# Three-pass split products for the attention and convolution output projections, LayerNorm on token rows, and another order of loading x, in an encoder kernel

## The chip, the cores and the metric

The kernel runs on one NeuronCore of a Trainium2 chip. The metric is the device time of one execution in microseconds (us); before the change it is 1177.25 us, the median of three runs (1176.48 to 1177.78). TensorE (PE) multiplies matrices and transposes; VectorE (DVE), ScalarE (ACT) and GpSimd (POOL) work element by element; SyncE (SP) and ACT issue DMAs here. Each engine takes its instructions in a fixed order. SBUF is the working memory, PSUM the memory into which PE writes; both have 128 partitions.

## The reference

Two layers over 256 tokens of width 1024, all in float32. One layer computes:

```
h = x + 0.5 * swiglu(rms_norm(x, norm_ffn1), w_ffn1_in, w_ffn1_out)
u = rms_norm(h, norm_mix)
q, k, v, c, g = split(u @ w_in)                 # 512, 128, 128, 1024, 2048 columns
y_attn = window_attention(norm(q), norm(k), v, sink, rel_bias) @ w_attn_out
c = c_val * sigmoid(c_gate)
c = depthwise_conv(c, conv_w) + conv_b          # 31 taps, 512 channels
c = silu(layer_norm(c, conv_ln_g, conv_ln_b))   # over the 512 channels of a token
y_conv = c @ w_conv_out
h = h + (sigmoid(g_attn) * y_attn + sigmoid(g_conv) * y_conv) @ w_o
h = h + 0.5 * swiglu(rms_norm(h, norm_ffn2), w_ffn2_in, w_ffn2_out)
x = h + (p @ w_pe_proj) * sigmoid(rms_norm(h, norm_pe) @ w_pe_gate)
```

The feed-forward width is 2816. The two matrices that the change touches, `w_attn_out` and `w_conv_out`, are 512 x 1024.

## The kernel before

Activations lie transposed: channels on the partitions, the 256 tokens along the free axis, so that a matrix with 1024 input channels is eight steps of 128 (k) and each product writes 128 output channels by 256 tokens.

Most matrices are multiplied in three passes of float32r (`mm3`): a weight and an activation are each held as a high part, the float32r rounding, and a low part, the rest, and high x high, high x low and low x high are added up in PSUM. The weights' parts are made on the way: `load_upto` issues the DMA of a unit of about 1 MB into one of four raw buffers (on SP, line L76 in the profile), and `prep_upto` casts a tile on ACT (`w_hi`, L100) and subtracts on DVE (`w_lo`, L101), into one of seven buffers each. Such a tile is 128 x 1024 and is called a spec. Preparation runs up to six specs ahead (`LOOK`), and a buffer comes free when PE has used it. The two output projections are the exception: their specs are raw (`raw_spec`), and `products` multiplies them in plain fp32.

The program text does not fix the order on the engines. A scheduler of the framework takes the instructions by priority on a modelled timeline and writes out one order per engine; the convolution's taps on DVE have a low priority (`BACKGROUND`), and the weights' preparation in the mixer has one between (`WEIGHTS_LAG`). In the first section of the program ACT and DVE keep the order of the text (`manual_schedule`).

The stages that the change touches:

- The start. x comes in four DMAs of 256 columns into `x_ld`, which is one of the four raw buffers. PE transposes it (`ps_xt`), ACT multiplies by the gain and rounds (`x0h`), DVE makes the rest (`x0l`), both engines copy it to `x32`. The gains come by a DMA of ACT into `rows_first` and through one more transposition (`ps_par`) into `par`. ACT squares `x32` block by block (`sq`), POOL adds the squares up (`sq_acc`), and a product with a constant matrix gives the mean square for all partitions (`ps_stat`). That product stands in PE's order among the first feed-forward products (`ps_gu`).
- The mixer's tail, once per layer. PE computes the gates (`ps_g`) while attention's scores, softmax and values are worked off between them and DVE runs the 124 convolution taps (L607, tile `y`). Then come four groups of the attention projection (`ps_ao`, each 256 output channels), four groups of the convolution projection (`ps_co`), and `w_o` (`ps_wo`). Between the `ps_ao` groups lies the LayerNorm of the convolution: a product with a constant matrix gives the mean (`ps_mu`), DVE subtracts it, ACT squares, a second product gives the variance (`ps_var`), then square root, reciprocal, product and Silu.

PSUM tiles named by `mm_tile` come from four buffers, those named by `at_tile` from two larger ones.

## Time and profile before

| what | number |
|---|---|
| median of three runs | 1177.25 us (1176.48 to 1177.78) |
| the profiled execution, its span | 1176.52 us, 1174.7 us |
| PE, DVE, ACT, POOL busy | 98%, 69%, 52%, 8% of the span |
| first `ps_gu` product | at 10.76 us |
| layer 0: first `ps_ao`, first `ps_co`, first `ps_wo` | at 313.55, 333.97 and 348.05 us |
| layer 1: first `ps_ao`, first `ps_co`, first `ps_wo` | at 889.83, 909.94 and 924.02 us |
| mean granted clock of TensorE | 0.999 |

In rows of the timeline the first number is the start in us from the span's start, the second the length; then engine, line, operation, tile written <- tiles read, shape, count, and in brackets the idle time before with what ended it. Rows of the windows give a stretch, its length, then busy time and count of PE, PE's weight loads, DVE, ACT and POOL, then granted clock, DMA share and GB/s. In a group of the page the busy sum and the mean in ns stand before the idle time. A busy PE is not PE at its peak: a matmul's record is longer than the distance to the next.

### The profile page before, as it was taken

Reading aid. Unit: us, or ns where it says so; the run is one execution under the profiler, and the core shown is the slowest. Engines: PE = TensorE matmul, PEld = TensorE weight load, DVE = VectorE, ACT = ScalarE, POOL = GpSimd, SP = SyncE. Lnnn points to the kernel's source line nnn. Section 1 sums busy time; section 2 is a strip of 40 time slices with the busy share of each in tenths; the row PEclk is TensorE's granted clock in tenths of the full one; section 3 lists DMA queues with packets and bytes.
Section 4 is the critical chain, followed back from the end, with each engine's and each line's share of the span. In section 5 each row is a group of like instructions: output and inputs, shape, how many; then the busy total and the mean of one; then the engine's idle time right before and its main releaser. Section 6 shows DMA issues by size and latency. Waiting matters only on the chain.

```text
span 1174.7 us, 21809 instructions
## 1 busy us (share of the span) xinstructions
PE 1156.8 (98%) x9082; PEld 1121.5 (95%) x9082; DVE 813.6 (69%) x1214; ACT 614.2 (52%) x1033; POOL 88.5 (8%) x119
## 2 busy tenths in 40 slices
PE   7999999999999999999999999999999999999997
PEld 7999999998889999999999999999987999999997
DVE  5866656798667766656876666569976786666564
ACT  6644444676356544444664444457753564444443
POOL 3000001211002000001110000113000010000110
PEclk9999999999999999999999999999999999999999
DMA  8866556545074565556556464566522664654541
GB/s 252 265 229 209 167 178 200 179 147 141 2 249 161 189 200 175 171 165 214 188 166 204 156 205 152 170 213 193 145 72 68 219 224 159 201 168 144 192 144 37
DMA packets 195694, 202.99 MB, mean 173 GB/s; under 512 B 3731, under 2 KB 188899, under 8 KB 195596
## 3 DMA queue, kind: packets, MB, share of 16 engines
q1 hardware_dynamic: 195564, 201.60, 53.6%
q8 instruction: 71, 1.16, 0.4%
q14 instruction: 27, 0.22, 0.1%
q10 hardware_dynamic: 32, 0.01, 0.0%
HBM read 200.53 MB, written 1.06 MB: 172 GB/s over the span
## 4 chain that ended last, share of the span: by engine, by line
PE 96%; DVE 2%; DMA 1%; ACT 1%; issue 0%; SPq 0%; ACTq 0%
PE ps_gu L313 14%; PE ps_gu L311 14%; PE ps_gu L312 14%; PE ps_fo L313 7%; PE ps_fo L312 7%; PE ps_fo L311 7%; PE ps_g L311 3%; PE ps_g L313 3%; PE ps_g L312 3%; PE ps_co L847 2%; PE ps_s L755 1%; PE ps_c L311 1%; PE ps_pe L313 1%; PE ps_pe L312 1%; PE ps_pe L311 1%; PE ps_c L313 1%
## 5 line engine op out<-in xcount | busy, mean ns | idle before, releaser
L101 DVE TENSOR_TENSOR w_lo<-raw,w_hi 128x1024 fp32r<-128x1024 f32 (+1 forms) x368 | 440.9, 1202 | 241.5 <-ACT w_hi L100 237.4
L100 ACT CAST w_hi<-raw 128x1024 fp32r<-128x1024 f32 (+1 forms) x368 | 377.2, 1030 | 427.0 <-PE ps_gu L312 215.3
L313 PE MATMUL ps_fo<-h_hi,w_lo 128*128 128x256 f32 x704 | 198.6, 283 | 0.0
L312 PE MATMUL ps_fo<-h_lo,w_hi 128*128 128x256 f32 x704 | 198.6, 283 | 0.0
L311 PE MATMUL ps_fo<-h_hi,w_hi 128*128 128x256 f32 x704 | 198.6, 283 | 0.0
L313 PEld LDWEIGHTS ps_fo<-h_hi,w_lo 128*128 128x128 f32 x704 | 134.9, 192 | 0.0
L311 PEld LDWEIGHTS ps_fo<-h_hi,w_hi 128*128 128x128 f32 x704 | 134.9, 192 | 0.0
L312 PEld LDWEIGHTS ps_fo<-h_lo,w_hi 128*128 128x128 f32 x704 | 134.9, 192 | 0.0
L400 POOL TENSOR_TENSOR sq_acc<-sq_acc,sq 128x256 f32<-128x256 f32 x56 | 56.5, 1010 | 903.4 <-ACT sq L399 902.9
L311 PE MATMUL ps_gu<-x0h,w_hi 128*128 128x256 f32 x352 | 100.8, 286 | 2.1 <-ACT x L456 2.1
L607 DVE SCALAR_TENSOR_TENSOR y<-cpad,cw,y 128x256 f32<-128x256 f32 x240 | 101.1, 477 | 0.1
L313 PE MATMUL ps_gu<-x0h,w_lo 128*128 128x256 f32 x352 | 100.4, 285 | 0.2 <-DVE w_lo L101 0.2
L312 PE MATMUL ps_gu<-x0l,w_hi 128*128 128x256 f32 x352 | 100.2, 285 | 0.0
L311 PE MATMUL ps_gu<-xn0h,w_hi 128*128 128x256 f32 x352 | 99.8, 284 | 0.0
L312 PE MATMUL ps_gu<-xf0l,w_hi 128*128 128x256 f32 x352 | 99.8, 284 | 0.0
L312 PE MATMUL ps_gu<-xf1l,w_hi 128*128 128x256 f32 x352 | 99.8, 284 | 0.0
L311 PE MATMUL ps_gu<-xf0h,w_hi 128*128 128x256 f32 x352 | 99.7, 283 | 0.0
L311 PE MATMUL ps_gu<-xf1h,w_hi 128*128 128x256 f32 x352 | 99.7, 283 | 0.0
L313 PE MATMUL ps_gu<-xf0h,w_lo 128*128 128x256 f32 x352 | 99.6, 283 | 0.0
L313 PE MATMUL ps_gu<-xn0h,w_lo 128*128 128x256 f32 x352 | 99.6, 283 | 0.0
L312 PE MATMUL ps_gu<-xn0l,w_hi 128*128 128x256 f32 x352 | 99.6, 283 | 0.0
L313 PE MATMUL ps_gu<-xf1h,w_lo 128*128 128x256 f32 x352 | 99.6, 283 | 0.0
(222 smaller groups left out, 2718.6 us busy)
## 6 DMA issues: line engine op xcount, KB each, us to landing
raw<-in_w_ffn_in_dram SPq DMA_DIRECT2D x86, 1024.0 KB
raw<-in_w_in_dram SPq DMA_DIRECT2D x30, 1024.0 KB
raw<-in_w_ffn_out_dram SPq DMA_DIRECT2D x32, 896.0 KB
raw<-in_w_ffn_out_dram SPq DMA_DIRECT2D x16, 1024.0 KB
raw<-in_w_o_dram SPq DMA_DIRECT2D x8, 1024.0 KB
raw<-in_w_pe_gate_dram SPq DMA_DIRECT2D x8, 1024.0 KB
raw<-in_w_attn_out_dram SPq DMA_DIRECT2D x8, 512.0 KB
raw<-in_w_conv_out_dram SPq DMA_DIRECT2D x4, 1024.0 KB
```

Of the source, the lines that this page charges most:

```text
L100: nc.scalar.copy(out=hv[:, :, d0 : d0 + w], in_=src),
L101: nc.vector.tensor_tensor(out=lv[:, :, d0 : d0 + w], in0=src, in1=hv[:, :, d0 : d0 + w].bitcast(F32), op=ALU.subtract,),
L311: nc.tensor.matmul(ps, wh[:, k0 + k, cols], xh[:, kx, :], start=f, stop=False)
L312: nc.tensor.matmul(ps, wh[:, k0 + k, cols], xl[:, kx, :], start=False, stop=False)
L313: nc.tensor.matmul(ps, wl[:, k0 + k, cols], xh[:, kx, :], start=False, stop=e)
L400: nc.gpsimd.tensor_tensor(out=self.acc, in0=self.acc, in1=sq, op=ALU.add)
L607: nc.vector.scalar_tensor_tensor(out=y[:, i, :], in0=src, scalar=w, in1=y[:, i, :], op0=ALU.mult, op1=ALU.add)
L755: nc.tensor.matmul(ps[:, c, :], qT[v * HD : (v + 1) * HD, c, qb * P : (qb + 1) * P], kT[v * HD : (v + 1) * HD, :], start=True, stop=True,)
L847: nc.tensor.matmul(ps[:, c * T : (c + 1) * T], w[:, k, c * P : (c + 1) * P], x[:, k, :], start=k == 0, stop=k == KC - 1,)
```

## The change

The two projections get split weights like all others, and their inputs are split as well: attention's output `o` when it leaves PSUM, the convolution's output after Silu (`y_h`, `y_l`). `products` calls `mm3`. LayerNorm goes by token rows: PE transposes `y` into two PSUM tiles of 128 tokens by 512 channels (`ps_yt`), DVE takes mean and variance per row (`bn_stats`, `bn_aggr`), normalises into `yn`, and PE transposes back (`ps_yc`), from where ACT applies Silu with gain and bias. It is called one attention group later in its second half (before the fourth instead of the third). At the start two of the four x loads are issued by ACT, two neighbouring k share a PSUM tile, the copies to `x32` come after the splits in pieces of 512, and the first weight spec is prepared after the fifth k. A scratch area of the DMA software is made smaller (1024), and the constant matrix of the mean is gone.

```diff
-        nc.sync.dma_start(x_ld[:, :, s], xv[:, :, s])
+        (nc.sync if i % 2 == 0 else nc.scalar).dma_start(x_ld[:, :, s], xv[:, :, s])
...
             for c in range(2):
-                ws.raw_spec(u, KC, c * 256, 256)
+                ws.spec(KC, 256, [(u, 0, c * 256, 0, 256)])
...
-        def keep_x(k):
-            copy = nc.scalar.copy if k % 2 else nc.vector.tensor_copy
-            copy(out=x32[:, k, :], in_=xT[k])
         for k in range(KD):
-            xT[k] = (mm_tile if 2 <= k < 6 else at_tile)("ps_xt")[:, :T]
+            if k % 2 == 0:
+                xT[k // 2] = mm_tile("ps_xt").rearrange("p (k t) -> p k t", k=2)
+            src = xT[k // 2][:, k % 2, :]
...
-            if k >= 2:
-                keep_x(k - 2)
-        ws.prep_upto(0)
-        keep_x(KD - 2)
-        keep_x(KD - 1)
+            if k == 4:
+                ws.prep_upto(0)
         ws.prep_upto(1)
+        for k in range(0, KD, 2):
+            copy = nc.scalar.copy if k % 4 else nc.vector.tensor_copy
+            copy(out=x32[:, k : k + 2, :], in_=xT[k // 2])
...
-                    nc.scalar.copy(out=o[:, :, qb * P : (qb + 1) * P], in_=ov[:, :, ::-1])
+                    split([p[:, :, qb * P : (qb + 1) * P] for p in o], ov[:, :, ::-1])
...
                 for c in range(2):
-                    for k in range(KC):
-                        nc.tensor.matmul(
-                            ps[:, c * T : (c + 1) * T], w[:, k, c * P : (c + 1) * P], x[:, k, :],
-                            start=k == 0, stop=k == KC - 1,
-                        )
+                    mm3(ps[:, c * T : (c + 1) * T], w, x, cols=slice(c * P, (c + 1) * P))
...
+            def ln_by_token():
+                mv = tmp.tile([P, 2, 2], F32, name="mv")
+                ps = []
+                for t in range(2):
+                    ps.append(mm_tile("ps_yt"))
+                    for i in range(KC):
+                        nc.tensor.transpose(ps[t][:, i * P : (i + 1) * P], y[:, i, t * P : (t + 1) * P], ident)
+                    six = tmp.tile([P, 6], F32, name="six")
+                    nc.vector.bn_stats(out=six, in_=ps[t])
+                    nc.vector.bn_aggr(out=mv[:, t, :], in_=six)
+                rs = tmp.tile([P, 2], F32, name="rs")
+                nc.scalar.activation(out=rs, in_=mv[:, :, 1], func=AF.Sqrt, bias=eps5)
+                nc.vector.reciprocal(out=rs, in_=rs)
+                table(AF.Silu)
+                for t in range(2):
+                    nc.vector.tensor_scalar(
+                        out=yn[:, t, :], in0=ps[t], scalar1=mv[:, t, 0:1], scalar2=rs[:, t : t + 1],
+                        op0=ALU.subtract, op1=ALU.mult,
+                    )
+
+            def ln_by_channel():
                 for i in range(0, KC, 2):
...
+                    ps = mm_tile("ps_yc").rearrange("p (f t) -> p f t", f=2)
+                    for f in range(2):
+                        for t in range(2):
+                            nc.tensor.transpose(
+                                ps[:, f, t * P : (t + 1) * P], yn[:, t, (i + f) * P : (i + f + 1) * P], ident
+                            )
+                    for f in range(2):
+                        nc.scalar.activation(
+                            out=y[:, i + f, :], in_=ps[:, f, :], func=AF.Silu,
+                            scale=pcol("conv_ln_g", l, i + f), bias=pcol("conv_ln_b", l, i + f),
+                        )
+                    split([p[:, i : i + 2, :] for p in yp], y[:, i : i + 2, :])
             for i in range(KC):
                 if i == 1:
-                    ln_mean()
-                if i == 2:
-                    ln_scale()
+                    ln_by_token()
+                if i == 3:
+                    ln_by_channel()
```

The scheduler's orders differ at three places.

ACT at the start, before (L180 loads the gains, L464 makes `x0h`, L456 copies to `x32`, L396 and L399 square):

```order
L180 DMA rows_first<-in_norm_ffn_dram 16x128
L191 ACT_TABLE_LOAD
L191 COPY par<-ps_par 128x16
L464 ACTIVATE x0h<-ps_xt,par 128x256 x4
L456 COPY x_99<-ps_xt 128x256
L464 ACTIVATE x0h<-ps_xt,par 128x256 x2
L456 COPY x_99<-ps_xt 128x256
L464 ACTIVATE x0h<-ps_xt,par 128x256 x2
L456 COPY x_99<-ps_xt 128x256
L100 CAST w_hi<-raw 128x1024
```

and now (L460 makes `x0h`, L469 copies):

```order
L166 DMA x_ld<-in_x_dram 128x2x256 x2
L180 DMA rows_first<-in_norm_ffn_dram 16x128
L191 ACT_TABLE_LOAD
L191 COPY par<-ps_par 128x16
L460 ACTIVATE x0h<-ps_xt,par 128x256 x5
L100 CAST w_hi<-raw 128x1024
L460 ACTIVATE x0h<-ps_xt,par 128x256 x3
L100 CAST w_hi<-raw 128x1024
L469 COPY x_97<-ps_xt 128x512
L100 CAST w_hi<-raw 128x1024 x2
L469 COPY x_97<-ps_xt 128x512
L394 ACTIVATE sq_acc<-x_97 128x256
```

Two loads of x stand ahead of the gains' load, the first cast stands after five `x0h` instead of eight, and four casts and the copies stand ahead of the first square, where two stood before. On PE `ps_par` now follows eight of the sixteen `ps_xt`, and the last two `ps_xt` stand after the first nineteen `ps_gu` products; the `ps_xt` of an odd k wait for the `x0l` of the even k in the same tile. On SP the DMA of the fourth weight unit waits for the first `w_lo`, and that of the fifth for the last `ps_xt`; before, it was the other way round.

DVE at the mixer's tail of layer 0, before (L607 are taps, L828 gates leaving PSUM, L857 an attention group leaving PSUM, L868 the subtraction of the mean):

```order
L828 TENSOR_TENSOR g<-ps_g,r_x 128x512
L607 SCALAR_TENSOR_TENSOR y<-cpad,cw,y 128x256 x6
L857 TENSOR_TENSOR g<-ps_ao,g 128x512
L607 SCALAR_TENSOR_TENSOR y<-cpad,cw,y 128x256 x2
L857 TENSOR_TENSOR g<-ps_ao,g 128x512
L868 TENSOR_TENSOR y<-y,ps_mu 128x512 x2
L101 TENSOR_TENSOR w_lo<-raw,w_hi 128x1024 x2
```

and now (L603 are taps, L849 an attention group):

```order
L101 TENSOR_TENSOR w_lo<-raw,w_hi 128x1024
L603 SCALAR_TENSOR_TENSOR y<-cpad,cw,y 128x256 x2
L849 TENSOR_TENSOR g<-ps_ao,g 128x512
L101 TENSOR_TENSOR w_lo<-raw,w_hi 128x1024
L603 SCALAR_TENSOR_TENSOR y<-cpad,cw,y 128x256 x17
L864 BN_STATS six<-ps_yt 128x6 x2
L865 BN_AGGR mv<-six 128x2 x2
L868 RECIPROCAL rs<-rs 128x2
L871 TENSOR_SCALAR yn<-ps_yt,mv,rs 128x512 x2
L849 TENSOR_TENSOR g<-ps_ao,g 128x512
L443 TENSOR_TENSOR y_l<-y,y_h 128x512
```

Seventeen taps now stand behind the third attention group, where none did. From the last `w_lo` of the gates on, the order has ten `w_lo` ahead of these taps; before, it had none between the gates' last and the taps' end.

PE at the same place, before (L847 are projection products in fp32, L866 and L876 mean and variance):

```order
L847 MATMUL ps_ao<-o,raw 128x256 x2
L866 MATMUL ps_mu<-y,ones_c 128x256
L876 MATMUL ps_var<-ysq,ones_c 128x256 x2
L847 MATMUL ps_ao<-o,raw 128x256 x9
L876 MATMUL ps_var<-ysq,ones_c 128x256 x2
L847 MATMUL ps_ao<-o,raw 128x256 x7
L847 MATMUL ps_co<-y,raw 128x256 x32
```

and now (L309 to L311 are the three passes of `mm3`; the first row ends the third attention group, and the rows after `ps_yc` begin the fourth):

```order
L311 MATMUL ps_ao<-o_h,w_lo 128x256
L862 MATMUL ps_yt<-ident,y 128x128 x4
L881 MATMUL ps_yc<-ident,yn 128x128 x2
L309 MATMUL ps_ao<-o_h,w_hi 128x256
L310 MATMUL ps_ao<-o_l,w_hi 128x256
```

The last four transposes of `y` and the first two of `yn` stand between the third and the fourth attention group; nineteen passes of the fourth group follow, then six more `ps_yc`, five more passes, and the 96 passes of `ps_co`.

More of the change, by code (lines that the diff above doesn't have):

```diff
@@ L267, in mix_specs @@
             for c in range(2):
[L268 removed]
+                ws.spec(KC, 256, [(u, 0, c * 256, 0, 256)])
         w = a["w_o"][l]
@@ L873, in ln_scale @@
[L873 to L884 removed]
+            yn = mp.tile([P, 2, CD], F32, name="yn", tag="sqq")
```

37 lines of the change are left out of this document (7 added, 30 removed).

## The prediction

> **What bounds the kernel now.** I read the page first.
>
> ```profile
> span 1174.7 us, 21809 instructions
> PE 1156.8 (98%) x9082; PEld 1121.5 (95%) x9082; DVE 813.6 (69%) x1214; ACT 614.2 (52%) x1033; POOL 88.5 (8%) x119
> PE 96%; DVE 2%; DMA 1%; ACT 1%; issue 0%; SPq 0%; ACTq 0%
> ```
>
> TensorE (PE) works through 98% of the span and carries 96% of the chain of waits. It is idle for 17.9 us in all. So only two things can move the end: fewer microseconds of PE work, or other microseconds of PE waiting. The profiled execution took 1176.52 us, 1.8 us more than its span and 0.7 us under the median of the three runs; the sum is made against it.
>
> The changed stages are the start and the two mixer tails. Layer 0's tail by windows, products of attention first, then of convolution:
>
> ```profile
> 313.55:333.97 20.42, 17.70 (x83) 14.93 (x81) 12.40 (x21) 7.97 (x10) 0.00 (x0) 1.00 0.27 88
> 333.97:348.05 14.08, 14.08 (x66) 12.43 (x67) 9.89 (x13) 6.98 (x9) 0.00 (x0) 1.00 0.88 287
> ```
>
> The first numbers are length and PE's busy time: 2.7 us of waiting in the first stretch, none in the second. The timeline names the waits and gives the pace:
>
> ```profile
> 313.55 3.62 PE L847 MATMUL ps_ao<-o,raw 128*128 128x256 f32 x16
> 323.95 1.13 PE L876 MATMUL ps_var<-ysq,ones_c 128*128 128x256 f32 x4 [1.61 <-ACT ysq L871]
> 333.97 14.08 PE L847 MATMUL ps_co<-y,raw 128*128 128x256 f32 x64 [1.11 <-ACT y L881]
> 301.06 0.66 PE ps_pt L792 x6
> 305.07 0.12 PE ps_g L313
> 348.05 0.35 PE ps_wo L311 x3
> ```
>
> 32 fp32 products stand as 64 records, 14.08 / 64 = 0.22 us each, so 0.44 us per product. A float32r pass takes 0.12 us, three of them 0.36.
>
> **The change, PE work alone.** Two matrices, two layers, 32 products each: 128 x (0.44 - 0.36) = 10.2 us less. LayerNorm trades 16 fp32 records per layer (0.22 us, 3.5 us) for 16 transposes of 128x128 (0.66 / 6 = 0.11 us each, as `ps_pt`): some 1.7 us less per layer. If nothing waited, that would be about 14 us gained. The order shows that something waits.
>
> **The mixer tail.** Before, VectorE (DVE) had only convolution taps left when attention's gates ended:
>
> ```profile
> 290.66:318.87 28.21, 22.28 (x53) 1.00 0.10 37
> L607 DVE SCALAR_TENSOR_TENSOR y<-cpad,cw,y 128x256 f32<-128x256 f32 x47 | 19.2, 477 | 0.1
> L828 DVE TENSOR_TENSOR g<-ps_g,r_x 128x512 f32<-128x512 f32 x4 | 2.8, 692 | 6.6 <-PE ps_g L313 6.6
> 306.55 4.83 DVE L607 SCALAR_TENSOR_TENSOR y<-cpad,cw,y 128x256 f32<-128x256 f32 x12
> 317.88 0.99 DVE L607 SCALAR_TENSOR_TENSOR y<-cpad,cw,y 128x256 f32<-128x256 f32 x2
> 328.14 2.36 DVE L101 TENSOR_TENSOR w_lo<-raw,w_hi 128x1024 fp32r<-128x1024 f32 x2 [4.30 <-ACT w_hi L100]
> ```
>
> In 28.21 us it ran 47 taps (0.40 us apart) and idled about 6, waiting for PE's gates; the last tap ended at 318.87. Now the eight weight tiles of the two projections are split too, and ten `w_lo` stand ahead of the last 17 taps: 8 projection tiles and the first two of `w_o`. At 2.36 / 2 = 1.18 us they add 11.8 us, one `o_l` 0.6, two more `ps_ao` evacuations 1.2 (row at 330.42, below, 0.6 from start to start): 13.6 us. If all idle time were filled, taps would end at 290.66 + 22.28 + 13.6 = 326.5; with the old idle time, at 332.5. The idle time is not free to fill, for the `w_lo` wait for casts on ScalarE (ACT), and those stand behind fixed work:
>
> ```profile
> 301.75 1.01 ACT L794 COPY pTs<-ps_pt 128x1024 f32<-128x1024 f32 x1 [5.21 <-PE ps_pt L792]
> 302.78 1.28 ACT L834 ACT_TABLE_LOAD   x1
> 304.08 2.95 ACT L834 ACTIVATE g<-g 128x1024 f32<-128x1024 f32 x3
> ```
>
> The fourth projection tile's cast stands behind the copy (done 302.8, so its `w_lo` starts at 303.9), the fifth behind table and sigmoids (308.0, so 309.0); tiles six to ten each wait for PE to give back one of seven buffers, 24 passes (2.9 us) apart. Walking the DVE order through these times, the tenth `w_lo` ends near 324.7 and the 17 taps, the last three dependent on each other at 0.5 us, near 331.9. I take 331.9.
>
> PE's order has no work to cover this. From 313.55 it has three groups of 24 passes and four transposes: 3 x 2.88 + 0.44 = 9.1 us, to 322.6. Next stand the last `ps_yt` transposes (need the last tap), then `ps_yc` (needs the normalised rows), and only behind them the fourth attention group. Queued behind the waiting transpose are also all convolution products and `w_o`; PE stands still for about 9.3 us. The work after the last tap:
>
> ```profile
> 7.32 0.90 ACT L464 ACTIVATE x0h<-ps_xt,par 128x256 fp32r<-128x256 f32 x2 [0.65 <-PE ps_xt L461]
> 330.42 0.68 DVE L857 TENSOR_TENSOR g<-ps_ao,g 128x512 f32<-128x512 f32 x1
> L782 DVE RECIPROCAL den<-den 128x4 f32<-128x4 f32 x1 | 0.2, 170 | 0.0
> L421 ACT ACTIVATE sd_tok<-ps_stat,eps 128x4 f32<-128x4 f32 x2 | 0.5, 256 | 0.0
> 333.31 1.58 ACT L881 ACTIVATE y<-y,par 128x256 f32<-128x256 f32 x3 [1.17 <-DVE y L880]
> 348.09 0.62 ACT L444 CAST ym_h<-g 128x512 fp32r<-128x512 f32 x1 [2.57 <-DVE g L909]
> ```
>
> Two transposes 0.5; two bn_stats over 128x512 from PSUM, 0.6 each, priced as the `ps_ao` row; two bn_aggr 0.17 each, as the small reciprocal (the trace has neither: between 0.1 and 0.7 us each, so the four between 0.4 and 2.8; I take 1.55, by the nearest rows); square root 0.26, reciprocal 0.17; first normalisation 0.65: 3.1 us, to 335.0. Then two transposes 0.4, nineteen passes of the fourth group, three transposes 0.5, four Silu at 0.5 = 2.0, the cast `y_h` 0.62. The passes follow a pause of 9 us, and the trace's one example of that is the program's start:
>
> ```profile
> 14.04 0.41 PE L311 MATMUL ps_gu<-x0h,w_hi 128*128 128x256 f32 x1
> 14.47 0.28 PE L313 MATMUL ps_gu<-x0h,w_lo 128*128 128x256 f32 x1
> 14.59 0.28 PE L311 MATMUL ps_gu<-x0h,w_hi 128*128 128x256 f32 x1
> ```
>
> Passes stood 0.21 us apart up to 14.47 (two in the 0.43 us between the first rows) and 0.12 from there on, twelve slow ones since 11.74 (the granted clock reads 1.00 in every window), so a restart costs 12 x 0.093 = 1.1 us. The 1.1 us pause before `ps_co` cost no such thing (still 0.22 per record). For a restart after 9 us the bounds are 0 and 1.1; I take 1.1, nearest the start, and again for the 2.5 us before the convolution products. Nineteen passes are then 3.4 us, and the products begin at 335.0 + 0.4 + 3.4 + 0.5 + 2.0 + 0.6 = 341.9. 96 passes at 0.12 plus 1.1 are 12.6: `w_o` starts at 354.5 instead of 348.05. That is +6.5 us per layer, **+13.0 us**. Layer 1 has the same rows 576 us later. With taps at 326.5 and no slow passes it is 347.0, -1.0 per layer; with twice the price for the unseen operations, +8.
>
> The Trainium skill, "TensorE: Matmul & The Clock Gate", Part 1, says that the array falls to half its clock after an idle window of about 3.4 us and needs as long a busy one to recover. The start's rows agree in kind, with 2.6 us of slow passes. By that page each restart would be an estimated 1.7 us and the total about 2.4 us higher; no mid-kernel row shows it.
>
> **The start.** The rows of before:
>
> ```profile
> 2.74 11.00 SPq L76 DMA_DIRECT2D raw<-in_w_ffn_in_dram  x6
> 3.58 0.17 ACT L191 COPY par<-ps_par 128x16 f32<-128x16 f32 x1 [1.09 <-PE ps_par L190]
> 6.59 2.07 PE L461 MATMUL ps_xt<-ident,x_ld 128*128 128x128 f32 x8 [0.70 <-DMA x_ld<-in_x_dram]
> 7.83 0.48 DVE L465 SCALAR_TENSOR_TENSOR x0l<-ps_xt,par,x0h 128x256 fp32r<-128x256 f32 x1 [0.61 <-ACT x0h L464]
> 9.35 1.08 ACT L100 CAST w_hi<-raw 128x1024 fp32r<-128x1024 f32 x1
> 10.46 1.22 DVE L101 TENSOR_TENSOR w_lo<-raw,w_hi 128x1024 fp32r<-128x1024 f32 x1 [0.32 <-ACT w_hi L100]
> 11.74 0.58 PE L313 MATMUL ps_gu<-x0h,w_lo 128*128 128x256 f32 x1 [0.19 <-DVE w_lo L101]
> 14.35:24.31 9.96, 9.96 (x85) 9.96 (x85) 6.20 (x6) 7.48 (x11) 6.60 (x6) 1.00 1.08 346
> 20.47 4.13 ACT L100 CAST w_hi<-raw 128x1024 fp32r<-128x1024 f32 x4 [0.89 <-DMA raw<-in_w_ffn_in_dram]
> 19.34 2.29 POOL L400 TENSOR_TENSOR sq_acc<-sq_acc,sq 128x256 f32<-128x256 f32 x2 [0.21 <-ACT sq L399]
> 24.31 0.59 PE L409 MATMUL ps_stat<-sq_acc,ones_d 128*128 128x256 f32 x2
> ```
>
> Issuing x from SP and ACT saves up to 1 us of issue (SP's first weight issue began at 2.74, after four of x); the load of the gains moves behind ACT's two. But `ps_par` now stands behind transposes of all four pieces of x, so the gains, ready at 3.75, come after the last piece (6.59, or up to 1 us sooner): I put the first `x0h` at T = 7.0 (6.5 to 7.5; before 4.72). And two k share one PSUM tile: the odd k's transposes wait until DVE has read the even one. Each round (transposes 0.73, two `x0h` 0.90, last `x0l` 0.51) is 2.1 us in series. After T: first pair's half 1.0, two rounds to 5.3, first `w_hi` to 5.9, first `w_lo` to 7.1, nineteen passes to 10.3, the last transposes to 11.0, last `x0h` 11.5, second `w_hi` 12.55, its `w_lo` 13.8. PE then has 23 passes behind it, at T + 13.8 = 20.8; before, at 11.74 + 2.56 + 8 x 0.12 = 15.3. That is 5.5 us late.
>
> The x32 copies and squares now stand behind three or four casts, and the first 1 MB weight unit is issued only after the last transposes (T + 11.0; before, after the first `w_lo`, 11.68). At 346 GB/s a unit is 3.0 us: casts 4 and 5 to T + 17.9 and 20.2, casts 6 and 7 to 22.2, the fifth and sixth square 23.0, cast 8, the last square 24.5, and POOL's last addition (1.0 us each) T + 25.7. `ps_stat` stands after 96 passes, which PE reaches at T + 22.6; it waits 3.2 us, everything behind it on PE too, and runs at 32.8 instead of 24.31: **+8.5 us**. PE never idles in the feed-forward stages, so nothing gives this back. Bounds: +4.5 (T = 6.0, no statistics wait) to +10.
>
> The smaller scratch size has no instruction. Sum: 1176.5 + 13.0 + 8.5 = **1198.0 us**.
>
> **Rivals.** (A) The start hides its part (0.14): x lands a microsecond sooner and the casts keep up, leaving about +1: 1176.5 + 13 + 1 = 1190. For it: ACT and DVE idle at the start; against: the waits are in series. (B) The tail is neutral (0.12): DVE fills its idle time, taps end near 326.5 and PE stays at pace: 1176.5 + 8.5 - 2 = 1183. For it: the 6 us of idle; against: the casts' places on ACT. (C) Faster (0.07): PE's work decides, because taps end before PE reaches the last `ps_yt` at 322.6. It needs DVE to end 9 us sooner than walked, below the no-idle bound of 326.5. It gives -13.6 of work, -5.4 of removed waits, -1 at the start: 1156.5. (D) Each pause restarts PE slowly, also those inside the start and after `ps_stat` (0.07): 1198 + 4 = 1202.
>
> **Chances and range.** The forecast has 0.58, A to D 0.40, and 0.02 lie near no change. About 0.2% is what a measurement of this kernel can tell. Faster 0.07, same 0.02, slower 0.91. The range 1184 to 1206 takes in A and D and the bounds of the unseen prices, and stops near B.
>
> **What would show it.** Right: PE idle about 9 us per layer before `ps_yt`, released by DVE's `y`; taps ending some 9 us after the third attention group; passes of 0.21 us behind the gap; `ps_stat` waiting for POOL, near 32 us; odd `ps_xt` released by DVE; feed-forward stages of the old length. Wrong: `w_o` starting less than 35 us after the first `ps_ao`, `ps_stat` before 26 us, or the last tap ahead of the third group's end.

## The result, and the profile after

The changed kernel takes **1197.12 us** (median of four runs, 1195.49 to 1199.37), the kernel before 1177.3 us on the same chip (1176.48 to 1177.78): a ratio of 1.017, with a 95% interval of 1.0151 to 1.019, so some 20 us slower. The profiled execution, at 1199.37 us the slowest of the four, has a span of 1197.6 us against 1174.7, 22.9 us more. The time is the forecast one; the way to it is only half the forecast one.

From the page after: the span and the busy times.

```profile
span 1197.6 us, 22131 instructions
PE 1143.8 (96%) x9210; PEld 1112.1 (93%) x9210; DVE 837.2 (70%) x1236; ACT 628.5 (52%) x1047; POOL 89.6 (7%) x118
```

PE is busy 13.0 us less than before, and idle for 53.8 us instead of 17.9. The work became less, the waiting grew by 35.9 us. PE's longest waits say where (what waits and what ended the wait; us in total, times, longest):

```profile
PE ps_yt L862 <- DVE y L603: 17.5, 4, 7.5
PE ps_yc L881 <- DVE yn L871: 5.7, 2, 2.9
PE ps_xt L457 <- DMA x_ld<-in_x_dram: 5.1, 2, 4.8
PE ps_xt L457 <- DVE x0l L461: 4.2, 3, 1.5
PE ps_co L309 <- ACT y_h L442: 4.1, 2, 2.6
PE ps_stat L407 <- POOL sq_acc L398: 3.1, 1, 3.1
PE ps_gu L310 <- DVE xf1l L431: 2.6, 2, 1.6
PE ps_gu L310 <- DVE xf0l L431: 2.3, 2, 1.4
```

All but the last two were forecast, and the wait for the first loads is nearly the old one (before, 1.1 us for x and 3.3 us for the gains). To see what each is worth, I set the start of the same product in both timelines side by side. The difference grows by what the stretch before it lost:

| first product of | before, us | after, us | behind by | so the stretch cost |
|---|---|---|---|---|
| `ps_stat` of the start | 24.31 | 35.48 | +11.2 | start |
| `ps_fo`, layer 0, first feed-forward | 141.76 | 154.18 | +12.4 | start, with what follows `ps_stat`: +12.4 |
| `ps_c` | 205.12 | 214.03 | +8.9 | down stage: -3.5 |
| `ps_ao` | 313.55 | 322.44 | +8.9 | 0 |
| `ps_wo` | 347.70 | 365.79 | +18.1 | tail: +9.2 |
| `ps_stat` behind the mixer | 375.75 | 398.67 | +22.9 | first gate and up group: +4.8 |
| `ps_pp` | 561.52 | 580.94 | +19.4 | down stage: -3.5 |
| `ps_gu`, layer 1 | 590.74 | 608.61 | +17.9 | embedding: -1.6 |
| `ps_c`, layer 1 | 781.24 | 795.59 | +14.4 | down stage: -3.5 |
| `ps_wo`, layer 1 | 923.67 | 946.63 | +23.0 | tail: +8.6 |
| `ps_stat` behind the mixer | 951.72 | 979.14 | +27.4 | +4.5 |
| `ps_pp`, layer 1 | 1137.50 | 1161.41 | +23.9 | down stage: -3.5 |
| `ps_out` | 1152.32 | 1175.48 | +23.2 | embedding: -0.8 |

(`ps_wo` before has a single product at 347.70, a third of a microsecond ahead of the row that the prediction quotes; both columns take the first one.) Start +12.4, tails +17.8, the stage behind each mixer +9.3, down stages and embedding -16.4. Two of these four sums are not in the prediction.

**The tail** in windows, before and after, from the first `ps_ao` to the first `ps_wo`:

```profile
313.55:347.70 34.15, 31.43 (x147) 27.04 (x145) 21.93 (x32) 14.95 (x18) 0.00 (x0) 1.00 0.51 167
322.44:365.79 43.35, 30.21 (x210) 28.83 (x209) 30.07 (x53) 15.61 (x19) 0.00 (x0) 0.80 0.28 89
```

DVE's busy time goes from 21.9 to 30.1 us, PE's falls, and the granted clock goes from 1.00 to 0.80. DVE's and PE's timeline after (rows left out at the dots and between):

```profile
332.62 1.23 DVE L101 TENSOR_TENSOR w_lo<-raw,w_hi 128x1024 fp32r<-128x1024 f32 x1 [0.24 <-ACT w_hi L100]
333.76 7.18 DVE L603 SCALAR_TENSOR_TENSOR y<-cpad,cw,y 128x256 f32<-128x256 f32 x17
341.51 1.29 DVE L864 BATCH_NORM_STATS2 six<-ps_yt 128x6 f32<-128x512 f32 x2 [0.57 <-PE ps_yt L862]
342.72 0.30 DVE L865 BATCH_NORM_AGGREGATE mv<-six 128x2 f32<-128x6 f32 x2
...
331.28 0.28 PE L311 MATMUL ps_ao<-o_h,w_lo 128*128 128x256 f32 x1
339.04 0.69 PE L862 MATMUL ps_yt<-ident,y 128*128 128x128 f32 x2 [7.48 <-DVE y L603]
341.00 0.69 PE L862 MATMUL ps_yt<-ident,y 128*128 128x128 f32 x2 [1.27 <-DVE y L603]
344.54 0.66 PE L881 MATMUL ps_yc<-ident,yn 128*128 128x128 f32 x2 [2.86 <-DVE yn L871]
345.22 0.42 PE L310 MATMUL ps_ao<-o_l,w_hi 128*128 128x256 f32 x1
345.43 0.41 PE L311 MATMUL ps_ao<-o_h,w_lo 128*128 128x256 f32 x1
352.43 0.73 PE L309 MATMUL ps_co<-y_h,w_hi 128*128 128x256 f32 x4 [1.54 <-ACT y_h L442]
```

The tenth `w_lo` ends at 333.8, the 17 taps behind it at 340.9, and PE stands still from 331.6 to 339.0. Behind the gap the passes are 0.21 us apart.

**The start**, after:

```profile
7.94 0.47 ACT L460 ACTIVATE x0h<-ps_xt,par 128x256 fp32r<-128x256 f32 x1
8.98 0.69 PE L457 MATMUL ps_xt<-ident,x_ld 128*128 128x128 f32 x2 [1.29 <-DVE x0l L461]
24.25 5.00 POOL L398 TENSOR_TENSOR sq_acc<-sq_acc,sq 128x256 f32<-128x256 f32 x4 [22.65 <-ACT sq L397]
31.36 4.07 POOL L398 TENSOR_TENSOR sq_acc<-sq_acc,sq 128x256 f32<-128x256 f32 x3 [2.11 <-ACT sq L397]
35.48 0.87 PE L407 MATMUL ps_stat<-sq_acc,ones_d 128*128 128x256 f32 x2 [3.06 <-POOL sq_acc L398]
```

**Behind the mixer** PE now waits for the low half of x, and **the down stage** (three passes of eight times 22 products, 528 passes) is shorter:

```profile
391.94 0.39 PE L310 MATMUL ps_gu<-xf0l,w_hi 128*128 128x256 f32 x1 [1.40 <-DVE xf0l L431]
```

```profile
141.76:205.12 63.36, 63.36 (x530) 63.36 (x529) 37.80 (x41) 29.51 (x40) 6.01 (x6) 1.00 0.59 194
154.18:214.03 59.85, 59.85 (x530) 59.85 (x529) 37.73 (x41) 29.59 (x40) 6.06 (x6) 1.00 0.64 205
```

The first row is of before, the second of after: the same 528 passes at 63.36 / 528 = 0.1200 us and at 59.85 / 528 = 0.1133 us, both at a granted clock of 1.00. Nothing in the program's text of this stage was changed.

### The profile page after: what moved, and what is told of

It is laid out like the page before. It is cut to its first block, busy times and chain, and to the rows that moved or that the text cites. A ratio compares the mean times of both kernels' runs of the same rounds, so it can differ in the third digit from the quotient of the medians.

```text
span 1197.6 us, 22131 instructions
## 1 busy us (share of the span) xinstructions
PE 1143.8 (96%) x9210; PEld 1112.1 (93%) x9210; DVE 837.2 (70%) x1236; ACT 628.5 (52%) x1047; POOL 89.6 (7%) x118
## 3 DMA queue, kind: packets, MB, share of 16 engines
q8 instruction: 72, 1.18, 0.4%
HBM read 200.53 MB, written 1.06 MB: 168 GB/s over the span
## 4 chain that ended last, share of the span: by engine, by line
PE 92%; DVE 5%; ACT 2%; DMA 1%; POOL 1%; issue 0%; ACTq 0%; POOLq 0%; DVEq 0%
PE ps_gu L310 14%; PE ps_gu L311 14%; PE ps_gu L309 14%; PE ps_fo L309 7%; PE ps_fo L310 7%; PE ps_fo L311 7%; PE ps_g L309 3%; PE ps_g L311 3%; PE ps_g L310 3%; DVE w_lo L101 2%; PE ps_s L751 1%; PE ps_c L309 1%; PE ps_c L311 1%; PE ps_c L310 1%; PE ps_o L798 1%; PE ps_pe L310 1%
## 5 line engine op out<-in xcount | busy, mean ns | idle before, releaser
L100 ACT CAST w_hi<-raw 128x1024 fp32r<-128x1024 f32 (+1 forms) x384 | 394.9, 1032 | 438.1 <-PE ps_gu L310 229.6
L101 DVE TENSOR_TENSOR w_lo<-raw,w_hi 128x1024 fp32r<-128x1024 f32 (+1 forms) x384 | 463.3, 1209 | 225.2 <-ACT w_hi L100 224.0
L309 PE MATMUL ps_fo<-h_hi,w_hi 128*128 128x256 f32 x704 | 193.7, 276 | 0.0
L310 PE MATMUL ps_fo<-h_lo,w_hi 128*128 128x256 f32 x704 | 193.7, 276 | 0.0
L311 PE MATMUL ps_fo<-h_hi,w_lo 128*128 128x256 f32 x704 | 193.7, 276 | 0.0
L309 PEld LDWEIGHTS ps_fo<-h_hi,w_hi 128*128 128x128 f32 x704 | 131.9, 188 | 0.0
L310 PEld LDWEIGHTS ps_fo<-h_lo,w_hi 128*128 128x128 f32 x704 | 131.9, 188 | 0.0
L311 PEld LDWEIGHTS ps_fo<-h_hi,w_lo 128*128 128x128 f32 x704 | 131.8, 188 | 0.0
L309 PE MATMUL ps_gu<-x0h,w_hi 128*128 128x256 f32 x352 | 102.6, 292 | 1.3 <-ACT w_hi L100 1.3
L311 PE MATMUL ps_gu<-x0h,w_lo 128*128 128x256 f32 x352 | 102.0, 290 | 1.2 <-DVE w_lo L101 1.2
L603 DVE SCALAR_TENSOR_TENSOR y<-cpad,cw,y 128x256 f32<-128x256 f32 x240 | 103.0, 475 | 0.2
L309 PE MATMUL ps_gu<-xf0h,w_hi 128*128 128x256 f32 x352 | 100.5, 286 | 0.0
L309 PE MATMUL ps_gu<-xf1h,w_hi 128*128 128x256 f32 x352 | 100.4, 285 | 0.0
L311 PE MATMUL ps_gu<-xf0h,w_lo 128*128 128x256 f32 x352 | 100.2, 285 | 0.0
L311 PE MATMUL ps_gu<-xf1h,w_lo 128*128 128x256 f32 x352 | 100.2, 285 | 0.0
L309 PE MATMUL ps_gu<-xn0h,w_hi 128*128 128x256 f32 x352 | 99.8, 284 | 0.0
L311 PE MATMUL ps_gu<-xn0h,w_lo 128*128 128x256 f32 x352 | 99.6, 283 | 0.0
```

Source lines behind the costliest of these rows:

```text
L100: nc.scalar.copy(out=hv[:, :, d0 : d0 + w], in_=src),
L101: nc.vector.tensor_tensor(out=lv[:, :, d0 : d0 + w], in0=src, in1=hv[:, :, d0 : d0 + w].bitcast(F32), op=ALU.subtract,),
L309: nc.tensor.matmul(ps, wh[:, k0 + k, cols], xh[:, kx, :], start=f, stop=False)
L310: nc.tensor.matmul(ps, wh[:, k0 + k, cols], xl[:, kx, :], start=False, stop=False)
L311: nc.tensor.matmul(ps, wl[:, k0 + k, cols], xh[:, kx, :], start=False, stop=e)
L603: nc.vector.scalar_tensor_tensor(out=y[:, i, :], in0=src, scalar=w, in1=y[:, i, :], op0=ALU.mult, op1=ALU.add)
```

## The experiments

### The two halves apart

One kernel has only the new start, the other only the new projections and LayerNorm (with the smaller scratch).

```diff
 # e1_start_only: of the change's diff, only the part in the start
+        (nc.sync if i % 2 == 0 else nc.scalar).dma_start(x_ld[:, :, s], xv[:, :, s])
+                xT[k // 2] = mm_tile("ps_xt").rearrange("p (k t) -> p k t", k=2)
+            if k == 4:
+                ws.prep_upto(0)
...
 # e2_tail_only: all but that part
+                ws.spec(KC, 256, [(u, 0, c * 256, 0, 256)])
+            def ln_by_token():
+                    mm3(ps[:, c * T : (c + 1) * T], w, x, cols=slice(c * P, (c + 1) * P))
...
```

> Only the reordered loading of x and the start are changed; mixer tails as before. By the prediction's term (+8.5 us) 1186, with ps_stat at 32.8 us. By the changed kernel's own trace, where ps_stat runs at 35.5 us and half-clock passes follow its 3.1 us wait, +12.4 us: 1189.5, with every later stage of before's length. If later stages can give part of it back, below 1184.

> Only the three-pass projections, the token-row LayerNorm and the smaller scratch are changed; the start is before's. By the prediction's term (+13.0 us) 1190. By the changed kernel's trace, stage by stage: first attention product to first w_o pass +9.2 and +8.6, first gate and up group after each mixer +4.7 and +4.5, four down stages -3.5 each, gate of the embedding -1.6 and -0.7: about +10.5, 1188. If the shorter down stages belong to the start and not to this part, 1204.

Measured: start alone **1188.98 us** (ratio 1.0102, 1.0087 to 1.0117), the rest alone **1186.85 us** (1.0081, 1.0066 to 1.0096). The sum of both, +11.9 and +9.8, is 21.7 us; together they cost 20. In the profiled execution of the first (1190.32 us, the slowest of its four) every stage from the first `ps_fo` to the end comes 13.6 to 13.8 us later than before: no stage gives a late start back. `ps_stat` waits there too:

```profile
36.08 1.22 PE L409 MATMUL ps_stat<-sq_acc,ones_d 128*128 128x256 f32 x2 [4.76 <-POOL sq_acc L400]
```

Both times lie nearer to those that the changed kernel's trace gave (1189.5 and 1188) than to the prediction's (1186 and 1190): the start is dearer than forecast, the second part cheaper, for it holds the -16.4 us.

### The loading of x alone

```diff
-        nc.sync.dma_start(x_ld[:, :, s], xv[:, :, s])
+        (nc.sync if i % 2 == 0 else nc.scalar).dma_start(x_ld[:, :, s], xv[:, :, s])
```

> The kernel before, with x loaded on the queues of SyncE and ScalarE by turns and nothing else changed by hand; the load of the gains now stands behind two pieces of x, and ps_par behind eight transposes. First x0h as in the changed kernel at 7.9 instead of 4.7 us and everything behind it 3.2 us later: ps_stat at 27.5, 1180. Then the shared tile and the later casts are the other 9 of the 12 us of e1_start_only. If the late gains cause most of it: 1186 or more; if the start absorbs them: 1177.

Measured: **1180.36 us** (1.0028, 1.0016 to 1.0039), as the first theory said. `ps_par` runs at 7.47 us, `ps_stat` at 28.54, 1 us later than expected. So issuing two pieces of x ahead of the gains costs 3.4 us, and the shared PSUM tile with the later casts and copies the other 8.5 of the 11.9.

### LayerNorm alone, projections alone

```diff
 # t1_ln_only: the change's LayerNorm in the kernel before; raw_spec and fp32 products stay
-                    ln_mean()
+                    ln_by_token()
...
 # t2_proj_only: the change's split projections (and smaller scratch) in the kernel before; LayerNorm stays, y is split behind Silu
-                ws.raw_spec(u, KC, c * 256, 256)
+                ws.spec(KC, 256, [(u, 0, c * 256, 0, 256)])
...
+                    if i % 2:
+                        split([p[:, i - 1 : i + 1, :] for p in yp], y[:, i - 1 : i + 1, :])
```

> The kernel before with the token-row LayerNorm alone: projections stay fp32, the start stays. Its small tiles put h, xe and pT 64 bytes below the weights modulo 256, as in the changed kernel, so the down stages and the embedding should be 16 us shorter in all (3.5 us per down stage, 1.6 and 0.7). The LayerNorm itself: PE work -1.7 us per layer, waits about 3.5 us before ps_yc and ps_co instead of 2.7: about -0.9 per layer. 1177 - 16 - 2 = 1159, first ps_ao to ps_wo some 33.5 us (before 34.2). If the LayerNorm's chain is what stalls the changed kernel, that stretch is over 38 us and the time 1169 or more.

> The kernel before with the three-pass projections alone: LayerNorm by columns and the start stay, h stays at the weights' place (0.1200 us per pass). If the weight splits ahead of the taps cause the stall, PE waits 7 to 9 us before the last ps_mu in each layer, half clock follows, the wait for xf_l behind the mixer appears too: +8 to +10 and +4.6 per layer, 1177 + 25 to 29 = 1202 to 1206. If the stall needs the new LayerNorm, PE's work decides: 1177 - 10 = 1167.

Measured: LayerNorm alone **1158.31 us** (0.9839, 0.9827 to 0.9852), projections alone **1207.67 us** (1.026, 1.0246 to 1.0273), 1.7 us above the upper end of what was expected. The longest waits of PE in the second, then the longest of the first:

```profile
PE ps_mu L863 <- DVE y L607: 18.1, 4, 8.3
PE ps_co L311 <- ACT y_h L444: 6.0, 2, 3.0
```

```profile
PE ps_yc L886 <- DVE yn L876: 3.7, 2, 1.9
```

The old LayerNorm stalls for the last tap just as the new one does. What makes the taps late comes with the split projections. The new LayerNorm is a gain: its first `ps_ao` to first `ps_wo` takes 32.41 us in layer 0 (before 34.15) and 31.85 in layer 1 (34.00), and most of the 18.8 us lies in the down stages and the embedding, which are as short as in the changed kernel (-3.5 us for each of four, -1.6 and -0.8). PE's wait for the low half of x behind the mixer is there in `t2_proj_only` (2.4 and 2.5 us) and not in `t1_ln_only`: it too came with the split projections.

### Without the low halves of the projections' weights

In the changed kernel, the third pass uses `w_hi` in place of `w_lo`, and the subtraction is not made. The products with the low part of these weights are left out, so its output is not the wanted one; PE keeps every pass.

```diff
-            lo = self.w_pool.tile([P, KD * P], F32R, name="w_lo")
+            lo = hi if self.next_prep in self.only_hi else self.w_pool.tile([P, KD * P], F32R, name="w_lo")
...
```

> The changed kernel, but the third pass of the two projections streams against w_hi again and their eight w_lo per layer are not made: VectorE loses 9.4 us of work per layer, PE keeps every pass (left out: the products with the low part of these weights, so the output is less exact). Theory 1, the w_lo ahead of the taps cause the stall: taps end before PE reaches the last ps_yt, no wait of 7.5 us and no half clock there, first ps_ao to first ps_wo 34 to 36 us instead of 43.4, two layers -16: 1181; with the wait for xf_l behind the mixer gone too, 1172. Theory 2, the stall comes from the new LayerNorm's own chain or its place in PE's order: 1197.

Measured: **1186.46 us** (against 1197.12 with them), between the two theories and nearer the first. The tails shrink from 43.35 and 42.65 to

```profile
321.89:359.83 37.94, 30.64 (x210) 30.03 (x209) 22.07 (x37) 16.27 (x20) 0.00 (x0) 0.82 0.32 103
896.40:934.05 37.65, 29.99 (x211) 29.29 (x209) 22.09 (x37) 16.25 (x20) 0.00 (x0) 0.82 0.32 103
```

5.4 and 5.0 us less, not 8. DVE's order shows why the rest stays:

```profile
328.81 0.47 DVE L602 SCALAR_TENSOR_TENSOR y<-cpad,cw,y 128x256 f32<-128x256 f32 x1
329.33 1.23 DVE L100 TENSOR_TENSOR w_lo<-raw,w_hi 128x1024 fp32r<-128x1024 f32 x1
331.26 0.69 DVE L848 TENSOR_TENSOR g<-ps_ao,g 128x512 f32<-128x512 f32 x1 [0.70 <-PE ps_ao L310]
331.86 1.29 DVE L863 BATCH_NORM_STATS2 six<-ps_yt 128x6 f32<-128x512 f32 x2
333.07 1.21 DVE L100 TENSOR_TENSOR w_lo<-raw,w_hi 128x1024 fp32r<-128x1024 f32 x1
```

The taps end at 329.3, before PE is through with its third group; but now a `w_lo` of `w_o` and an evacuation stand between the last tap and the row statistics and a second `w_lo` right behind these, PE waits 4.5 us for `yn`, and the clock drops again (0.82). So the splits ahead of the taps are the main cause, shown by the run: without them the wait for the last tap is gone and more than half of the 9.2 and 8.6 us with it. The LayerNorm's chain behind them is the next in line. The wait for the low half of x behind the mixer stayed as well (2.4 us per layer), so its cause is not these eight splits; what in the split projections causes it stays open.

### The fourth attention group ahead of the wait

```diff
                 if i == 1:
                     ln_by_token()
-                if i == 3:
-                    ln_by_channel()
                 attn_out(2 * i)
                 if i == 0:
                     squash(12)
+            ln_by_channel()
```

> The changed kernel with the transposes back to channels written behind the fourth attention group instead of ahead of it, so PE runs all four groups before it waits for the last tap. The wait before the last ps_yt then starts 2.9 us later and the 19 passes of the fourth group no longer run at half clock behind it: some 4 us less per layer, 1197 - 8 = 1189. If another chain (weight splits, y_h) ends the tail anyway: 1197. The start and the wait behind the mixer stay as they are.

Measured: **1195.02 us** (1194.05 to 1197.16), 2 us less than the changed kernel, not 8; the spreads of the two overlap. The tails take 41.2 and 41.7 us instead of 43.4 and 42.7. PE does run its four groups first, to 335.4, but it still waits 6.7 us, for DVE is later by as much:

```profile
335.62 0.68 DVE L849 TENSOR_TENSOR g<-ps_ao,g 128x512 f32<-128x512 f32 x1
336.51 1.23 DVE L101 TENSOR_TENSOR w_lo<-raw,w_hi 128x1024 fp32r<-128x1024 f32 x1 [0.21 <-ACT w_hi L100]
337.65 6.40 DVE L603 SCALAR_TENSOR_TENSOR y<-cpad,cw,y 128x256 f32<-128x256 f32 x15
```

The fourth group gives its weight buffer back sooner, so an eleventh `w_lo` is ready and goes ahead of the last taps, with the fourth evacuation: 1.23 + 0.68 us more, and the last tap comes at 344.05 (1.06 of that is this run's later start) instead of 340.94. Here DVE is the bound, and most of the cover that PE finds by working ahead is eaten up by the DVE work that it sets free. My expectation had left that out.

### The pace of a pass

The down stage's shorter passes were the surprise. What differs there is the address: the LayerNorm's small tiles replace a larger one, and all tiles of the stage pools (`h`, `xe`, `pT`) lie 64 bytes lower against the weight tiles, counted modulo 256, than before. The smaller scratch is not it: `t1_ln_only` keeps the old scratch and has the short passes, `t2_proj_only` has the smaller one and keeps 0.1200. So I put unused bytes into the kernel before; the order on all engines stays the same but for a memset on POOL. `p1_pad_h` moves `h`, `xe`, `pT` up by 64 bytes, `p2_pad_x` the x tiles too, `p3_pad_all` all tiles with the weights.

```diff
-    col = {}
+    col, pad = {}, tmp.tile([P, 16], F32, name="pad", bufs=1); nc.gpsimd.memset(pad, 0.0)   # p1
+    col, pad = {}, xp.tile([P, 16], F32, name="pad"); nc.gpsimd.memset(pad, 0.0)            # p2
+    pad = const.tile([P, 16], F32, name="pad"); nc.gpsimd.memset(pad, 0.0)                  # p3, ahead of ident
+    col, pad = {}, xp.tile([P, 48], F32, name="pad"); nc.gpsimd.memset(pad, 0.0)            # p4
```

> The kernel before with 64 unused bytes per partition ahead of the tiles h, xe, pT (and all that the stage pools hold); same instructions in the same order, and one memset more on GpSimd. Theory 1: a float32r pass takes 0.1200 or 0.1133 us by where its moving tile starts modulo 128 bytes (before: 32, as the weights; changed kernel: 96). Then the four down stages are 3.5 us shorter each and the embedding about 1 us: 1161. Theory 2: the shorter passes come from something else in the change (scratch size, load on the engines): 1177, passes of ps_fo 0.1200 us apart.

> The kernel before with the same 64 unused bytes, but ahead of x32 and the normalised x tiles too; weights stay. Theory 1: the 5376 passes that stream x (gate and up, conv, gates of the mixer) also go from 0.1200 to 0.1133 us, 36 us more than the pad ahead of h alone: 1125, if ScalarE and VectorE split weights fast enough (24 passes take 2.72 us, one split pair 1.03 and 1.20 us); with waits for splits up to 1140. Theory 2 (address is not the cause): 1177.

Measured: **1170.62 us** (0.9947, 0.9932 to 0.9961) and **1159.64 us** (0.9854, 0.9837 to 0.987): faster, but by 6.4 and 17.4 us instead of 16 and 52. The same down stage takes

```profile
142.02:204.21 62.19, 62.19 (x530) 62.19 (x529) 37.86 (x41) 29.62 (x40) 6.05 (x6) 1.00 0.60 197
```

62.19 / 528 = 0.1178 us per pass, a third value beside 0.1200 and 0.1133. Alignment modulo 128, which I had assumed, is the same here as in the changed kernel (96), so it does not decide. But in `p2_pad_x` the products that stream weights against x as the held operand (`ps_kv`) had gone to 0.1136: there the streamed tile lies 64 bytes below the held one. So a fourth kernel puts x, h and xe 64 bytes below the weights, and the third tests that it is the distance.

What I had overlooked is that `p2_pad_x` has both paces with x 64 bytes above the weights. These rows stand around the `ps_stat` product behind layer 0's mixer:

```profile
366.75 0.28 PE L311 MATMUL ps_gu<-xf0h,w_hi 128*128 128x256 f32 x1
371.51 0.28 PE L311 MATMUL ps_gu<-xf0h,w_hi 128*128 128x256 f32 x1
371.63 0.59 PE L409 MATMUL ps_stat<-sq_acc,ones_d 128*128 128x256 f32 x2
372.18 0.28 PE L313 MATMUL ps_gu<-xf0h,w_lo 128*128 128x256 f32 x1
377.13 0.28 PE L313 MATMUL ps_gu<-xf0h,w_lo 128*128 128x256 f32 x1
```

From the first to the second row are 42 passes, from the fourth to the fifth as many: 4.76 / 42 = 0.1133 us each ahead of `ps_stat` and 4.95 / 42 = 0.1179 behind it, with the same tiles of x. So the sign of the distance alone does not decide between these two paces, though the next expectation assumes it.

> The kernel before with 192 unused bytes ahead of x32, the x tiles and everything behind them; weights stay at 160 modulo 256. The runs so far gave 0.1200 us per pass where the moving tile lies at the weights' place modulo 256, 0.1178 at 64 bytes above it, 0.1133 at 64 bytes below (h in the changed kernel, and the weights streamed against x in p2_pad_x). Here x, h, xe and pT all lie 64 below (96 against 160). If the distance decides: 0.1133 us for some 7900 passes, 0.0067 us less each, 1177 - 50 = 1127, or up to 1140 if the splits of weights cannot keep up. If 0.1133 was due to something else in the changed kernel (it also has another scratch size and other absolute addresses): 1160 like p2_pad_x, or 1177.

> The kernel before with 64 unused bytes ahead of all its tiles, so moving and stationary tiles shift together (all from 160 to 224 modulo 256). If the distance between moving and stationary tile decides the pace, passes stay 0.1200 us apart and the time 1177; if the address of the moving tile itself decides, they are 0.1178 us apart as in p2_pad_x, and the time is about 1160.

Measured: **1135.2 us** (0.9649, 0.9632 to 0.9666) and 1176.8 us (one run). Moving everything together changes nothing; moving the streamed tiles against the held ones gains 42 us. Two stretches of 14 us of `p4_pad192`, both of gate and up products of layer 0's first feed-forward, with the same tile of x:

```profile
25.40:39.40 14.00, 14.00 (x126) 14.00 (x125) 8.50 (x8) 7.14 (x8) 0.00 (x0) 1.00 0.63 192
60.00:74.00 14.00, 14.00 (x122) 14.00 (x120) 9.76 (x14) 6.83 (x10) 0.00 (x0) 1.00 0.54 175
```

Each count holds some two records that reach in over the edges; from start to start the passes are 0.1133 us apart in the first stretch and 0.1178 in the second. Between the two PE transposes the convolution's weights and runs other small products. The 0.1178 then lasts through the first down stage and the mixer of layer 0, the second feed-forward has 0.1133, and in layer 1's mixer 0.1178 comes back behind `ps_stat`. So a distance of 64 bytes rules out 0.1200 but leaves two paces; in the traces one gives way to the other where other work of PE stands between the passes, and what chooses stays open. Some 2100 passes of this execution are 0.1178 us apart; 2100 x 0.0045 = 9.5 us is about what parts 1135 from the expected 1127.

### The best of both

LayerNorm by token rows, with 48 and 16 unused floats that put x, h, xe and pT 64 bytes below the weights; fp32 projections and start of before.

> The kernel before with the token-row LayerNorm and with unused bytes that put x, h, xe and pT 64 bytes below the weights modulo 256; projections and start as before. The pad alone gave 1135.2 in p4_pad192; the LayerNorm is expected to take another 2 us: 1133. If the LayerNorm gains nothing: 1135; if its chain stalls PE: 1141 or more.

Measured: **1134.52 us** (0.9634, 0.961 to 0.9658; six executions from 1127.27 to 1140.22). It beats both kernels by far, but it cannot be told from the pad alone (1135.2): the LayerNorm's 2 us are lost in a spread of 13 us. The two paces above could make such a spread, but only one of the six executions was traced.

## Why the prediction was right or wrong, point by point

**PE's work alone** (-10.2 us for the products): right. The three attention groups with four transposes take 331.56 - 322.44 = 9.1 us, as worked out. PE is busy 13.0 us less, though that holds slow passes on one side and the shorter down stages on the other, so it does not prove the 10.2.

**The tail's mechanism**: right, step by step. Counted from the first `ps_ao`, the last tap was put at 331.9 - 313.55 = 18.4 us and came at 18.5; PE was to be through with its third group at 9.1 and was; the wait of 9.3 is 7.5 + 1.3 with transposes between. The unseen operations were priced well: a row statistic 0.65 us (0.6), its aggregation 0.15 (0.17). `t2_proj_only` and `t3_no_wlo` show that the splits ahead of the taps are the cause, and the walk through DVE's order was worth its length.

**The tail's size**: +6.5 per layer forecast, +9.2 and +8.6 measured. A third to half a microsecond of the difference is the row that was taken for the first `ps_wo`; the rest lies behind the last tap:

| step | forecast, us | layer 0 | layer 1 |
|---|---|---|---|
| first `ps_ao` to last tap | 18.4 | 18.5 | 18.5 |
| last tap to first `ps_yc` | 3.1 | 3.6 | 3.6 |
| first `ps_yc` to first `ps_co` | 6.9 | 7.9 | 8.3 |
| first `ps_co` to first `ps_wo` | 12.6 | 13.4 | 12.2 |

The term that was mis-sized most in layer 0 is the restart of PE ("a restart costs 12 x 0.093 = 1.1 us", taken twice): the 19 passes behind the gap and 17 of the first convolution products ran at 0.21 us, 36 x 0.093 = 3.3 us instead of 2.2. In layer 1 the second slow stretch did not come, and the two restarts cost less than forecast; there the cast of `y_h` stands behind a weight cast of 1.05 us. In both layers two transposes of `y` take 0.69 us at half pace, where 0.5 had been put. The twelve slow passes at the program's start were taken for the price of a restart, but PE was slow there before the first pass: the eight transposes of x in the prediction's row took 2.07 us, 0.26 each, against 0.11 for `ps_pt`. So the twelve show only the rest of a slow stretch. PE's granted clock after, window by window (the number behind the counts is the clock):

```profile
332.84:336.25 3.41, 0.00 (x0) 0.00 (x0) 3.41 (x8) 1.04 (x1) 0.00 (x0) 1.00 0.36 100
336.25:349.90 13.65, 6.73 (x29) 5.96 (x30) 7.79 (x18) 1.58 (x2) 0.00 (x0) 0.50 0.15 53
349.90:353.32 3.42, 1.88 (x14) 1.48 (x13) 1.38 (x2) 3.38 (x7) 0.00 (x0) 1.00 0.00 0
353.32:356.73 3.41, 3.41 (x17) 3.41 (x18) 1.83 (x2) 0.52 (x2) 0.00 (x0) 0.50 0.02 5
```

The clock is halved for 13.65 = 4 x 3.41 us, whole for one such window, halved for another (in layer 1 it is halved once, from 916.5 to 930.2). The Trainium skill, "TensorE: Matmul & The Clock Gate", Part 1, says that activity is judged in free-running windows of 3413 ns and that a window of full work brings the clock back; the trace agrees with both. The prediction gave the price by the Trainium skill beside its own and used the row of the start; that estimate (1.7 us for each restart) is the nearer one in layer 0, where two restarts cost 3.3 us.

**The start**: mechanism right, size off, +8.5 forecast and +12.4 measured. The rounds of 2.1 us are 2.17, and PE's wait of 3.2 us for POOL is 3.1. Three terms were too small: T is 7.94 instead of 7.0, since the first transposes wait for x until 4.83 us and the eight ahead of `ps_par` end at 7.30, and the weight load of `ps_par` behind them has waited 0.5 us for the gains, third on ACT's queue (`s1_load_only` prices the loading by turns at 3.4 us in all); POOL's last addition ends at T + 27.5 instead of T + 25.7, with additions of 5.00 / 4 = 1.25 and 4.07 / 3 = 1.36 us that had been put at 1.0; and after `ps_stat` the clock is halved for 3.4 us, which costs the step from +11.2 to +12.4. (It was halved from 22.2 to 25.6 us as well, but that is covered: PE still reached `ps_stat` 3.1 us ahead of POOL.) The Trainium skill, "SBUF — State Buffer", Who interferes with whom, says that a DVE instruction with two SBUF inputs contends with a POOL instruction that reads SBUF; the weight splits run there at the same time and the last four take 5.82 / 4 = 1.46 us each instead of 1.18, so the slower additions agree with it, but no run here shows it alone.

**"PE never idles in the feed-forward stages, so nothing gives this back"**: right for the late start, which `e1_start_only` carries to the end undiminished, and wrong for the whole change, on both sides; "feed-forward stages of the old length" did not come about. The first gate and up group behind each mixer loses 4.8 and 4.5 us: PE waits 2.3 and 2.6 us for the low half of x, and a window at half clock follows. The down stages and the embedding give 16.4 us back by their pace, which the prediction had as a constant. The two errors, with 3.9 us too little for the start and 4.8 for the tails, cancel: 13.0 + 8.5 forecast is 21.5, and 12.4 + 17.8 + 9.3 - 16.4 is 23.1 (profiled; 20 by the medians). **The number was right partly by luck.**

**The rivals.** (A), a start that hides its part, and (B), a tail without a wait, did not come about; even without the `w_lo` the tail is 3.7 us longer than before's. (C), PE's work decides, did not come about either: `t1_ln_only` comes near its time, but most of that gain is the pace of the passes, not fewer or cheaper ones. (D), each pause restarts PE slowly, held 0.07 and names part of what the forecast's sum lacked: a slow stretch follows `ps_stat`, another the waits behind each mixer, and layer 0's tail has two.

## What to carry to other kernels

A cheaper form of a product can cost its gain on another engine: here 10 us of PE work went, and 9.4 us of weight splits per layer arrived on DVE, just ahead of the last link of the chain that PE waits for. Add up what an edit puts ahead of the latest producer in that engine's order before counting what it saves on the busiest one. And when a stage changes its length that no edit touches, look at where its tiles lie: an edit that frees or adds a few hundred bytes moves every tile behind it.

## What the runs showed of the hardware

**The pace of a float32r pass of 128x256 changes with where the streamed tile lies against the held one.** Addresses are those that the program assigns, modulo 256 bytes:

| streamed tile, kernel | streamed minus held | us per pass |
|---|---|---|
| x, h, before; x, after; all, `p3_pad_all` | 0 | 0.1200 |
| h, `p1_pad_h` | +64 | 0.1178 |
| x and h, `p2_pad_x` | +64 | 0.1178; ahead of `ps_stat` in the start and behind each mixer 0.1133 |
| h, xe, after and `t1_ln_only`; weights in `ps_kv`, `p2_pad_x` | -64 | 0.1133 to 0.1136 |
| x, h, `p4_pad192` and `b1_pad_ln` | -64 | 0.1133, in long stretches 0.1178 |

On some 7900 passes the step from 0.1200 to 0.1133 would be 50 us, more than the whole change. Page "SBUF — State Buffer" of the Trainium skill, in the same section as above, says that TensorE never waits on anyone and reads streamed and held operand through two independent ports; by that the distance should not matter, and here the measurement decides. Other distances were not tried, and what chooses between 0.1133 and 0.1178 is open.

**The clock falls without a wholly idle window.** The Trainium skill, "TensorE: Matmul & The Clock Gate", Part 1, has the clock fall after an idle window of about 3.4 us; less is enough here. The next two rows, of after, are a window with PE busy for 1.32 of 3.42 us and the halved one behind it; the third is a window with 1.67 us busy, behind which the clock stayed whole:

```profile
390.86:394.28 3.42, 1.32 (x7) 0.92 (x7) 3.42 (x7) 1.30 (x3) 0.72 (x1) 1.00 1.08 345
394.28:397.69 3.41, 3.41 (x16) 3.41 (x17) 1.87 (x2) 1.60 (x3) 1.13 (x1) 0.50 0.33 108
930.16:933.58 3.42, 1.67 (x14) 1.46 (x13) 0.69 (x1) 2.63 (x5) 0.00 (x0) 1.00 0.00 0
```

All halved stretches of this execution begin on one grid of 3.413 us and, but for the one that the end cuts off, last whole multiples of it. On this grid, behind the first 15 us (where the clock reads 1.00 while PE runs at half pace), every window at full clock with PE busy for 41% or less was followed by a halved one; 49% and more was not, but for 55% once (from 349.90, quoted above, like the 49% right behind a halved stretch). So the border lies near half a window here. In layer 0 two waits of 1.4 and 0.9 us in one window halved the next, and the first gate and up products up to `ps_stat` took 9.84 us instead of 5.16, 2.4 us more than the waits last; a wait of 2.6 us across two windows in layer 1 (before `ps_co`) halved nothing. The price of a pause hangs on where it falls in the grid.
